# Attention: group 0's heads split behind block 1 of group 2, into places of used keys; input blocks 0 to 3 into places of the normed input

## The chip, the cores and the metric

The kernel runs on one core of a Trainium2 chip. The metric is the device time of one execution in microseconds (us). Before the change three runs took 1659.44, 1661.74 and 1659.78 us; the median is 1659.78 us.

The engines are named as in the profile: PE multiplies matrices (PEld is its weight load), DVE works on vectors, ACT computes functions of one argument and copies, POOL and SP issue DMAs here. Each engine runs its instructions in the order of its own program and waits on semaphores for the others.

## The reference

The program is the trunk of an encoder of two layers, over 768 tokens (512 of one request, 256 of another) of width 1024.

```python
for i in range(DEPTH):                      # 2 layers
    h = rms_norm(x, norm_mix[i])
    x = x + (window_attention(h, ...) if i % 2 == 0 else short_conv(h, ...))
    h = rms_norm(x, norm_mlp[i])
    x = x + jnp.square(jax.nn.relu(h @ mlp_w_up[i])) @ mlp_w_down[i]
    gate = jax.nn.sigmoid(rms_norm(x, norm_ple[i]) @ ple_w_gate[i])
    x = x + (p[i] @ ple_w_proj[i]) * gate
return rms_norm(x, final_norm)
```

`window_attention` has 16 heads in 4 groups with shared keys and values, each query sees the keys within 128 tokens, with a bias and a sink logit; its output is multiplied by `w_o`. The change touches the attention of layer 0, its output product and what follows it; `p[1] @ ple_w_proj[1]` of layer 1 is computed early, right behind that output product.

## The kernel before

**Numbers in two parts.** Every product is computed in fp32r from operands in two parts: `split(hi, lo, src)` writes the high part on ACT (L84) and the rest, `src - hi`, on DVE (L85). A term of a product is three matmuls: high weight by high input, high weight by low input, low weight by high input.

**Places.** Tokens lie along the free dimension, so a block of 128 channels is a tile of 128x768, 384 KB. Such tiles lie in numbered places, `slot(i, name)`. Taking a place again waits until the tile that had it before was last used. During the attention the places hold: 0, 1, 4, 8 the high and 2, 3, 5, 9 the low parts of the keys of groups 0 to 3 (`khh`, `kll`); 16 to 23 the high and 24 to 31 the low parts of the normed input (`xs_mix`), which the query products read; later the high (16 to 23) and low (24 to 31) parts of the attention's output, the split heads (`aos`); and 0 to 7 the eight blocks of the input x (`xa`), onto which the output product is added.

**Attention.** `attend(g)` runs over the groups g = 0 to 3 and in each over six blocks n of 128 queries. For a block: scores S on PE (L725, L726), bias and maximum on DVE (L727), exponential on ACT (L747), transposes `pt` (L760), probabilities in two parts `ph` (ACT, L768) and `pl` (DVE, L769), products O with the values (L770, L771), and the sum into `heads[g]` (DVE, L778). In this stage a scheduler sets the order of each engine's instructions from the order in which the program issues them and the times it reckons with. The table `beside` says which other work is issued behind block n of group g: query products for the heads to come (`queries(c)`), keys, layer 1's input, and, at (2, 4), `begin_output`: the heads of groups 0 and 1 are split. At (2, 5) `first_output` loads the first four blocks `xa` (L799) and forms the output products of groups 0 and 1 (matmuls L140 into `mm`, added by DVE at L794).

**Behind the attention.** `first_head` forms the output products of groups 2 and 3 for the eight blocks (matmuls L131), six of them in its loop in the order 4, 0, 5, 1, 6, 2, and adds each onto its block `xa[m]` to give x (DVE, L869). `first_tail` does blocks 7 and 3 and then the four products `pj` of layer 1's p (`product(m)`, L131). Their inputs, p in two parts for k = 0 and 1 (`p1`, the profile says `p`), are split in `second_inputs`: `behind(0)` and `behind(1)` take the places `xs0[24:]`, that is 16, 17 (high and low for k = 0), 18 and 19 (k = 1). Behind them comes the first MLP (L1096 and on), with products formed in seven multiplications in place of eight (L486). From `first_tail` on, PE, DVE and ACT keep the order in which the program is written.

Of the kernel before, what the change touches and what calls it, by code (L numbers as in the profile page):

```python
# [11 lines left out]
F32 = mybir.dt.float32  # L12
# [35 lines left out]
def trunk_kernel(ctx: ExitStack, tc: tile.TileContext, a: dict, out: bass.AP):  # L48
# [33 lines left out]
    def split(hi, lo, src):  # L82

        first = act.activation(hi, src, AF.Copy)  # L84
        dve.tensor_tensor(lo, src, hi.bitcast(F32), ALU.subtract)  # L85
        return first.ins
# [6 lines left out]
    def weight(src, n, raw=None, tag="w"):  # L93

        m = CH if src is None else src.shape[1]
        if raw is None:
            raw = fetch(src)
        pool, bufs = (wp, 2) if tag == "w" else (more, 1)
        hi, lo = (pool.tile([P, CH], F32R, tag=f"{tag}{p}", name=f"{tag}{p}", bufs=bufs) for p in ("hi", "lo"))
        split(hi[:, :m], lo[:, :m], raw[:, :m])  # L100
        return blocks(hi[:, :m], n), blocks(lo[:, :m], n)
# [48 lines left out]
    def slot(i, name, dt=F32R, n=T):  # L150

        return (slots if i < 32 else more).tile([P, n], dt, tag=f"S{i}", name=name)

    def big(name, dt=F32):

        nonlocal turn
        if more is None:
            return tmp.tile([P, T], dt, tag="t", name=name)
        turn += 1
        return tmp.tile([P, T], dt, tag=f"q{turn % 6}", name=name, bufs=1)  # L160

    def terms_of(w, xs, col=0):

        hi, lo = w
        c = slice(col, col + P)
        return [(wh[:, c], wl[:, c], xh, xl) for wh, wl, xh, xl in zip(hi, lo, *xs)]
# [324 lines left out]
    def mixer_attention():  # L491
# [25 lines left out]
        def products(terms):  # L517

            if not split_products:
                ps = psum.tile([P, 1024], F32, tag="mm", name="mm")  # L520
                group(ps, terms)
                yield ps[:, :T], 0, T
                return
            o = 0
            for i, n in enumerate(SEQS):
                ps = psum.tile([P, 512], F32, tag=f"mm{i}", name="mm", bufs=BM)
                group(ps, [(wh, wl, xh[:, o : o + n], xl[:, o : o + n]) for wh, wl, xh, xl in terms], n)
                yield ps[:, :n], o, o + n
                o += n
# [14 lines left out]
        with tc.manual_schedule(engines=order):  # L544
# [21 lines left out]
            hi = wp.tile([P, CH], F32R, name="whi", bufs=2)  # L566
            lo = wp.tile([P, CH], F32R, name="wlo", bufs=2)
# [25 lines left out]
        with s1:  # L593
# [29 lines left out]
            def queries(c):  # L623
                w = wq[0] if c == 0 else weight(a["w_q"][c], KB, raw=wq[1] if c == 1 else None)
                t = big("qt")
                for ps, o, e in products(terms_of(w, xs)):
                    dve.scalar_tensor_tensor(t[:, o:e], ps, HD**-0.5, r[:, o:e], ALU.mult, ALU.mult)
                hi = big("qh", F32R)
                lo = big("ql", F32R)
                split(hi[:], lo[:], t[:])  # L630
                for j in range(2):
                    h = 2 * c + j
                    qst[h] = slot(QS[h % 8], "q")
                    for i, part in enumerate((hi, lo)):
                        nc.sync.dma_start(
                            qst[h][64 * i : 64 * i + 64, :].bitcast(F32),
                            part[64 * j : 64 * j + 64, :].bitcast(F32),
                        )
# [11 lines left out]
            for i, raw in enumerate(rawv):  # L650

                m = min(T, 2 * CH - i * T)
                hi, lo = slot((4, 8, 10)[i], "wvh"), slot((5, 9, 11)[i], "wvl")
# [26 lines left out]
            aos = [], []  # L680
            xa = {}
# [100 lines left out]

            def split_heads(g):
                for i in range(2):
                    hi, lo = (slot(16 + 8 * p + 2 * g + i, "aos") for p in range(2))
                    split(hi[:], lo[:], heads[g][:, i, :])
                    aos[0].append(hi[:])
                    aos[1].append(lo[:])
# [6 lines left out]

            def load_part(m0):
                for m in range(m0, m0 + 4):
                    xa[m] = slot(m, "xa", F32)
                    nc.sync.dma_start(xa[m][:], a["x"][m])  # L799

            def first_output():
                load_part(0)
                for j in range(2):
                    w = weight(a["w_o0"][j], 4)
                    for i in range(2):
                        output_part(2 * j + i, w, i * P)

            def second_output():
                split_heads(2)
                load_part(4)  # L810
                for m in range(4, KB):
                    output_part(m, weight(a["w_o1"][m - 4], 6))
# [6 lines left out]
            def projected(n):  # L819
                if n == 0:  # L820
                    projw.append(weight(a["proj"][1, 0], 2))
                for m in range(2 * n, 2 * n + 2):
                    step(1, m, projw[0], part1, "t", False)
# [8 lines left out]
                    for p in range(2):  # L832
                        part1[p].append(ps[p][:, k, :])

            def begin_output():
                for g in range(2):
                    split_heads(g)


            beside = {  # L840
                (0, 5): (inputs1, keys1),
                (1, 4): (lambda: projected(0),),
                (1, 5): (lambda: projected(1),),
                (2, 4): (begin_output,),
                (2, 5): (first_output,),
            }
            for g in range(KV - 1):
                for n in range(2):
                    beside[g, 1 + 2 * n] = (lambda c=2 * g + 2 + n: queries(c),)
            for g in range(KV):  # L850
                attend(g)
            second_output()
            split_heads(3)
        return xa, aos

    xa, aos = mixer_attention()
    psum = ctx.enter_context(tc.tile_pool(name="ps", bufs=8, space=PSUM))
    more = ctx.enter_context(tc.tile_pool(name="more", bufs=1))
# [1126 lines left out]
```

## Time and profile before

| | |
|---|---|
| median of three runs | 1659.78 us |
| profiled execution, device time | 1661.51 us |
| its span in the trace | 1659.5 us |
| mean granted clock of PE over the span | 0.996 |
| busy: PE, DVE, ACT | 1637.6, 1380.8, 948.5 us |

The span runs from the first to the last instruction of the trace; 2.0 us of the device time lie around it. In rows of the timeline the columns are start (us), duration, engine, line, operation, tile written and tiles read, and in brackets the engine's idle time ahead of it with what ended it. Rows of windows give the stretch, its length, the busy time of each engine with the number of instructions, PE's granted clock (1.00 is full), the busy share of the DMA engines and GB/s. Rows of waits give who waited for whom: total us, times, the longest. The attention with the output products of groups 0 and 1 lies before 260 us, `first_head` and `first_tail` from about 268 to 303 us.

### The profile page before, as it was taken

To read this page: it belongs to the slowest core of one execution; us is meant where nothing else is said; L and a number is where in the kernel's file an instruction comes from. 1 tells how busy PE (TensorE), PEld (TensorE's weight loads), DVE (VectorE), ACT (ScalarE), POOL (GpSimd) and SP (SyncE) were. 2 spreads that over 40 slices of the span, in tenths; PEclk is the share of its full clock that TensorE was granted. 3 is DMA by queue.
4 is the path that set the end of the run, shared out by engine and by line. 5 is a ranking of instruction groups with operands and counts; after the bars stand their busy time and mean duration, and the time that the engine had idled before them with its cause. 6 is when DMAs were issued, how large, how long until landed. Compare 5 with 4: busy or idle time off the path is not lost.

```text
span 1659.5 us, 24297 instructions
## 1 busy us (share of the span) xinstructions
PE 1637.6 (99%) x9414; PEld 1587.3 (96%) x9414; DVE 1380.8 (83%) x2242; ACT 948.5 (57%) x1508; POOL 71.7 (4%) x104
## 2 busy tenths in 40 slices
PE   8999999999999999999999999999999999999997
PEld 7988789999999999999999999999999999999986
DVE  7598888898889889877888777778889888988776
ACT  7377766865556556545654434555555655655554
POOL 0211000000000000000000000000000000000000
PEclk9999999999999999999999999999999999999998
DMA  8755322443233333242312222112333323333222
GB/s 267 199 154 149 87 64 83 121 109 87 83 86 96 96 96 91 71 122 69 98 62 77 76 77 76 64 64 73 87 96 96 95 87 79 90 96 108 69 87 99
DMA packets 55476, 161.11 MB, mean 97 GB/s; under 512 B 7056, under 2 KB 10128, under 8 KB 55360
## 3 DMA queue, kind: packets, MB, share of 16 engines
q1 hardware_dynamic: 45184, 139.89, 26.4%
q0 software_dynamic: 10176, 19.67, 6.7%
q8 instruction: 74, 1.21, 0.3%
q14 instruction: 42, 0.34, 0.1%
HBM read 138.82 MB, written 10.48 MB: 90 GB/s over the span
## 4 chain that ended last, share of the span: by engine, by line
PE 88%; DVE 7%; ACT 4%; issue 1%; DMA 0%; DVEq 0%; SPq 0%; ACTq 0%
PE a L486 33%; PE mm L131 10%; PE mm L140 8%; PE b L486 8%; PE d L486 5%; PE c L486 5%; PE B L486 4%; PE C L486 4%; PE gate L140 3%; PE pt L760 1%; PE p L1096 1%; PE p L1199 1%; PE gate L131 1%; PE O L770 1%; PE O L771 1%
## 5 line engine op out<-in xcount | busy, mean ns | idle before, releaser
L486 PE MATMUL a<-xs,whi 128*128 128x384 f32 x624 | 121.8, 337 | 0.0
L444 ACT ACTIVATE vhi<-wraw 128x512 fp32r<-128x512 f32 x67 | 42.2, 631 | 132.3 <-PE B L486 87.9
L486 PEld LDWEIGHTS a<-xs,whi 128*128 128x128 f32 x624 | 110.0, 188 | 0.2 <-DVE y L1306 0.2
L486 PE MATMUL a<-t,zhi 128*128 128x384 f32 x536 | 109.1, 337 | 0.0
L486 PE MATMUL a<-t,whi 128*128 128x384 f32 x536 | 108.8, 336 | 0.0
L486 PE MATMUL b<-t,zhi 128*128 128x384 f32 x536 | 108.7, 336 | 0.0
L1341 DVE TENSOR_TENSOR x<-x,a 128x384 f32<-128x384 f32 x112 | 62.1, 554 | 55.3 <-PE a L486 55.3
L486 PE MATMUL a<-act,whi 128*128 128x384 f32 x448 | 96.5, 337 | 0.0
L486 PEld LDWEIGHTS a<-t,whi 128*128 128x128 f32 x536 | 94.9, 188 | 0.0
L486 PEld LDWEIGHTS b<-t,zhi 128*128 128x128 f32 x536 | 94.9, 188 | 0.0
L486 PEld LDWEIGHTS a<-t,zhi 128*128 128x128 f32 x536 | 94.8, 188 | 0.0
L464 DVE TENSOR_TENSOR wlo<-wraw,whi 128x1024 fp32r<-128x1024 f32 x70 | 85.2, 1218 | 7.9 <-ACT whi L444 7.9
L444 ACT ACTIVATE whi<-sum 128x1024 fp32r<-128x1024 f32 x67 | 70.6, 1054 | 27.0 <-PE a L486 22.7
L464 DVE TENSOR_TENSOR wlo<-sum,whi 128x1024 fp32r<-128x1024 f32 x67 | 81.8, 1220 | 5.1 <-ACT whi L444 5.1
L1058 ACT ACTIVATE y<-y 128x768 f32<-128x768 f32 x64 | 53.7, 839 | 54.4 <-DVE y L1055 54.3
L464 DVE TENSOR_TENSOR zlo<-sum,zhi 128x1024 fp32r<-128x1024 f32 x67 | 81.5, 1217 | 0.0
L140 PE MATMUL mm<-xs_mix,whi 128*128 128x512 f32 (+1 forms) x320 | 81.0, 341 | 0.0
L486 PEld LDWEIGHTS a<-act,whi 128*128 128x128 f32 x448 | 79.8, 188 | 0.0
L444 ACT ACTIVATE whi<-wraw 128x1024 fp32r<-128x1024 f32 x72 | 75.7, 1051 | 7.0 <-PE C L486 7.0
L444 ACT ACTIVATE zhi<-sum 128x1024 fp32r<-128x1024 f32 x67 | 70.9, 1058 | 11.9 <-DVE sum L420 11.0
L486 PE MATMUL a<-xs,wlo 128*128 128x384 f32 x312 | 67.1, 336 | 0.0
L358 ACT ACTIVATE t<-y 128x768 fp32r<-128x768 f32 x56 | 45.7, 838 | 34.9 <-DVE y L349 34.4
(345 smaller groups left out, 4558.4 us busy)
## 6 DMA issues: line engine op xcount, KB each, us to landing
wraw<-in_up SPq DMA_DIRECT2D x64, 512.0 KB, 3.9
wraw<-in_down SPq DMA_DIRECT2D x64, 512.0 KB, 4.2
wraw<-in_w_in SPq DMA_DIRECT2D x24, 512.0 KB, 3.5
wraw<-in_gate SPq DMA_DIRECT2D x16, 512.0 KB, 3.4
vlo<-in_up POOLq DMA_DIRECT2D x28, 256.0 KB, 5.6
vlo<-in_down POOLq DMA_DIRECT2D x28, 256.0 KB, 6.0
pj<-pjs SPq DMA_DIRECT2D x16, 384.0 KB, 2.8
wraw<-in_w_q SPq DMA_DIRECT2D x8, 512.0 KB, 4.6
```

Of the source, the lines that this page charges most:

```text
L131: pe.matmul(t, lhsT=w, rhs=x[:, o:e], start=first and i == 0 and j == 0, stop=last and i == n - 1 and j == 2)
L140: pe.matmul(ps[:, o:e], lhsT=w, rhs=x[:, o:e], start=i == 0 and j == 0, stop=i == n - 1 and j == 2,)
L358: act.activation(t[0][:], (self.q1, self.q2)[i][:], AF.Copy)
L444: act.activation(hi[:], src, AF.Copy)
L464: dve.tensor_tensor(lo[:], src, hi[:].bitcast(F32), ALU.subtract)
L486: pe.matmul(ps, lhsT=a, rhs=b, start=start and i == 0, stop=i == len(terms) - 1, skip_group_check=True)
L760: pe.transpose(pt[:, h * P : (h + 1) * P], lg[h // 2][:, h % 2, b * P : (b + 1) * P], ident[:],)
L770: pe.matmul(O[:], lhsT=v, rhs=ph[:], start=b == 0, stop=False)
L771: pe.matmul(O[:], lhsT=v, rhs=pl[:], start=False, stop=b == nk - 1)
L1058: act.activation(t[:], t[:], AF.Square)
L1096: pe.matmul(ps[o], lhsT=wt[:, c], rhs=xs[f"x{h + 1}{1 + o}"][m][part], start=k == 0 and j == 0, stop=k == KB - 1 and j == 2,)
L1341: dve.tensor_tensor(t[:, o : o + H], t[:, o : o + H], f, op)
```

## The change

Three edits. The split heads of group 0 go into places 0 and 1 (high) and 2 and 3 (low), those of the keys of groups 0 and 1, in place of 16, 17, 24 and 25. The blocks `xa[0]` to `xa[3]`, which had the places 0 to 3, go into 24, 25, 16 and 17. And group 0's heads are split by an entry of `beside` at (2, 1), behind `queries(6)`, and no longer at (2, 4), where group 1's stay. Lines behind L835 have numbers lower by 3 in the changed kernel.

```diff
             def split_heads(g):
                 for i in range(2):
-                    hi, lo = (slot(16 + 8 * p + 2 * g + i, "aos") for p in range(2))
+                    hi, lo = (slot(2 * p + i if g == 0 else 16 + 8 * p + 2 * g + i, "aos") for p in range(2))
                     split(hi[:], lo[:], heads[g][:, i, :])
...
             def load_part(m0):
                 for m in range(m0, m0 + 4):
-                    xa[m] = slot(m, "xa", F32)
+                    xa[m] = slot((24, 25, 16, 17, 4, 5, 6, 7)[m], "xa", F32)
                     nc.sync.dma_start(xa[m][:], a["x"][m])
...
-            def begin_output():
-                for g in range(2):
-                    split_heads(g)
-
...
-                (2, 4): (begin_output,),
+                (2, 4): (lambda: split_heads(1),),
                 (2, 5): (first_output,),
             }
             for g in range(KV - 1):
                 for n in range(2):
                     beside[g, 1 + 2 * n] = (lambda c=2 * g + 2 + n: queries(c),)
+            beside[2, 1] += (lambda: split_heads(0),)
```

How it moves instructions is seen at three places. First PE, where the output products begin, in group 2 of the attention. `aos_2502`, `2503`, `2506` and `2507` are the high and low parts of group 0's heads before, `aos_2236`, `2237`, `2240` and `2241` the same after; 2510 to 2515 are group 1's. Before:

```order
L771 MATMUL O_2344<-pl_2362,vv_457 128x512
L725 MATMUL S_2520<-khh_1388,q_1609 128x256
L726 MATMUL S_2520<-kll_1389,q_1609 128x256
L725 MATMUL S_2524<-khh_1388,q_1612 128x256
L726 MATMUL S_2524<-kll_1389,q_1612 128x256
L725 MATMUL S_2529<-khh_1388,q_1813 128x256
L726 MATMUL S_2529<-kll_1389,q_1813 128x256
L140 MATMUL mm_2594<-aos_2507,whi_2590 128x512
L140 MATMUL mm_2594<-aos_2506,wlo_2591 128x512
L140 MATMUL mm_2594<-aos_2510,whi_2590 128x512
```

After the change:

```order
L140 MATMUL mm_2594<-aos_2240,whi_2590 128x512
L140 MATMUL mm_2594<-aos_2241,whi_2590 128x512
L140 MATMUL mm_2594<-aos_2240,wlo_2591 128x512
L140 MATMUL mm_2594<-aos_2510,whi_2590 128x512
L725 MATMUL S_2463<-khh_1388,q_1816 128x256
L726 MATMUL S_2463<-kll_1389,q_1816 128x256
L140 MATMUL mm_2594<-aos_2511,whi_2590 128x512
L725 MATMUL S_2520<-khh_1388,q_1609 128x256
L726 MATMUL S_2520<-kll_1389,q_1609 128x256
L140 MATMUL mm_2594<-aos_2510,wlo_2591 128x512
```

Before, three pairs of scores stand ahead of the product with `aos_2507`; after, the product with `aos_2241` is in that run's place and scores and products alternate. Second, DVE early in the attention, where one of group 0's splits goes (piece of the difference):

```order
 L627 SCALAR_TENSOR_TENSOR qt<-mm,rstd_mix_428 128x512
 L755 TENSOR_SCALAR L<-L,sm 128x256 x3
+L85 TENSOR_TENSOR aos<-heads,aos 128x768
 L627 SCALAR_TENSOR_TENSOR qt<-mm,rstd_mix_428 128x256
 L769 TENSOR_TENSOR pl<-pt,ph 128x512 x2
```

The other goes some 100 instructions further on, ahead of the sums `sm`; where all four splits of groups 0 and 1 stood, group 1's two remain. Third, DVE in `first_head`, where the low part of `p1` for k = 0 (`p1_3369`) was written. Before:

```order
L794 TENSOR_TENSOR xa_3121<-xa_3121,mm_3267 128x512
L85 TENSOR_TENSOR zlo_3342<-wraw_3339,zhi_3341 128x1024
L85 TENSOR_TENSOR p1_3369<-wraw_3366,p1_3368 128x768
L794 TENSOR_TENSOR xa_3121<-xa_3121,mm_3287 128x256
L85 TENSOR_TENSOR wlo_3375<-wraw_3372,whi_3374 128x1024
```

After, in `first_tail`, where `xa_2586` is `xa[3]` and `xs7` and `x12` are the normed input of the MLP:

```order
L199 TENSOR_TENSOR acc_mlp0_3331<-acc_mlp0_3331,sq_3655 128x768
L866 TENSOR_TENSOR x_3328<-xa_2586,mm_3567 128x384
L866 TENSOR_TENSOR x_3328<-xa_2586,mm_3568 128x384
L85 TENSOR_TENSOR p1_3369<-wraw_3366,p1_3368 128x768
L308 SCALAR_TENSOR_TENSOR xs7_3668<-x_3328,vec_76,xs7_3668 128x384
L308 SCALAR_TENSOR_TENSOR x12_3669<-x_3328,vec_76,x12_3669 128x384
```

The split of `p1_3369` stands some 35 instructions later, behind the last add of the stage. On PE the products `pj` keep their place behind the output product of block 3; the first two read `p1_3368`, the next two `p1_3369`.

## The prediction

> **What bounds the kernel now.** I read the page first, then TensorE's waits over the whole run, then windows around the two stretches that the change touches.
>
> ```profile
> span 1659.5 us, 24297 instructions
> ...
> PE 1637.6 (99%) x9414; PEld 1587.3 (96%) x9414; DVE 1380.8 (83%) x2242; ACT 948.5 (57%) x1508; POOL 71.7 (4%) x104
> ...
> PE 88%; DVE 7%; ACT 4%; issue 1%; DMA 0%; DVEq 0%; SPq 0%; ACTq 0%
> ```
>
> PE is busy 99% of the span and carries 88% of the chain that ended last. The change leaves the number of instructions on every engine as it is, so only PE's idle time and PE's clock can move the end. All waits of PE together are few; these three stand in or near the stretches in question:
>
> ```profile
> PE mm L140 <- DVE aos L85: 1.6, 1, 1.6
> ...
> PE O L770 <- DVE heads L778: 0.4, 1, 0.4
> PE b L486 <- DVE zlo L464: 0.4, 1, 0.4
> ```
>
> The longest is PE waiting for the split of the heads (`aos`), once, for 1.6 us. Two-microsecond windows around it:
>
> ```profile
> 192.00:194.00 2.00, 2.00 (x16) 1.78 (x15) 2.00 (x6) 2.00 (x6) 0.00 (x0) 1.00 0.00 0
> 194.00:196.00 2.00, 2.00 (x15) 1.75 (x14) 2.00 (x6) 2.00 (x4) 0.00 (x0) 1.00 0.00 0
> 196.00:198.00 2.00, 1.58 (x13) 1.26 (x11) 1.96 (x6) 1.95 (x5) 0.00 (x0) 1.00 0.59 128
> 198.00:200.00 2.00, 1.84 (x6) 0.93 (x6) 2.00 (x7) 1.94 (x4) 0.00 (x0) 1.00 0.97 241
> 200.00:202.00 2.00, 0.93 (x6) 0.59 (x4) 1.88 (x7) 0.89 (x3) 0.00 (x0) 1.00 0.43 109
> 202.00:204.00 2.00, 1.52 (x4) 1.23 (x5) 2.00 (x3) 1.70 (x9) 0.00 (x0) 0.56 0.80 309
> 204.00:206.00 2.00, 2.00 (x9) 1.71 (x8) 2.00 (x11) 0.51 (x1) 0.00 (x0) 0.59 0.00 0
> ```
>
> Columns: length, then busy time of PE, PEld, DVE, ACT, POOL with counts, then PE's clock, the DMA share and GB/s. Two things are to be seen. PE idles 0.42 + 0.16 + 1.07 + 0.48 = 2.13 us between 196 and 204, while DVE is full from 192 to 206: here DVE is the bound. And the clock falls. Cut where it falls:
>
> ```profile
> 198.83:202.24 3.41, 2.10 (x9) 1.16 (x8) 3.29 (x12) 2.23 (x6) 0.00 (x0) 1.00 0.66 181
> 202.24:205.66 3.42, 3.18 (x9) 2.60 (x10) 3.42 (x12) 1.97 (x7) 0.00 (x0) 0.50 0.39 152
> ```
>
> After a stretch in which PE was idle for 1.3 of 3.41 us comes one of equal length at half clock, in which 3.18 us of PE's work took twice its time: 1.6 us lost. So what stands to be won here is about 2.13 + 1.6 = 3.7 us.
>
> **Part 1: group 0's heads split earlier (gain).**
>
> ```profile
> L85 DVE TENSOR_TENSOR aos<-heads,aos 128x768 fp32r<-128x768 f32 x4 | 3.6, 954 | 0.0
> ...
> 193.30 0.96 DVE L85 TENSOR_TENSOR aos<-heads,aos 128x768 fp32r<-128x768 f32 x1
> ...
> 201.47 2.69 DVE L85 TENSOR_TENSOR aos<-heads,aos 128x768 fp32r<-128x768 f32 x3
> ...
> 202.48 0.79 PE L140 MATMUL mm<-aos,whi 128*128 128x512 f32 x1 [1.56 <-DVE aos L85]
> ```
>
> Four low-part splits of 0.95 us each fall into 193 to 204, three of them back to back at 201.47, and PE resumes at 202.48 when the first of those three is done. After the change two of the four leave this stretch. In the new order they stand where DVE and ACT idle today:
>
> ```profile
> 123.00 0.51 ACT L747 ACTIVATE L<-L,nm 128x256 f32<-128x256 f32 x1 [1.11 <-DVE nm L740]
> ...
> 128.70 0.42 DVE L627 SCALAR_TENSOR_TENSOR qt<-mm,rstd_mix 128x256 f32<-128x256 f32 x1 [1.25 <-PE mm L140]
> ...
> 163.01 0.59 ACT L773 ACTIVATE ot<-O 64x512 f32<-64x512 f32 x1 [1.04 <-PE O L771]
> ...
> 173.14 0.69 DVE L627 SCALAR_TENSOR_TENSOR qt<-mm,rstd_mix 128x512 f32<-128x512 f32 x1 [1.73 <-PE mm L140]
> ```
>
> ACT's half of a split (0.84 us) fits its 1.11 and 1.04 us of idle, DVE's 0.95 us fits 1.25 and 1.73. I cost them at nothing there; without that cover each would hold the transposes behind it by up to 1 us. At 196 to 204 PE gets products of group 0 that wait for nothing, laid between its score products, and the idle before 202.48 goes. What is late next is DVE's own work there. From DVE's side the gain is 2 x 0.95 = 1.9 us, plus 1.6 if the clock then holds: 3.5. From PE's side it is at most 3.7. Following the new PE order with the durations of before, I come to 3.3, a score product still waiting about a microsecond for DVE to empty its bank. I take **-3.3**; ends -1.9 (the clock still falls) and -3.7.
>
> **Part 2: the first four input blocks are loaded later (nothing).**
>
> ```profile
> 188.07 0.40 PE L140 MATMUL mm<-xs_mix,whi 128*128 128x256 f32 x2
> ...
> DMA to landing us min/median/max: 3.1/3.7/6.9
> ...
> 195.64 0.46 SPq L635 DMA_DIRECT2D q<-qh  x1
> ...
> 207.19 0.68 DVE L794 TENSOR_TENSOR xa<-xa,mm 128x512 f32<-128x512 f32 x1
> ```
>
> The new places were held by the normed input, last read by the query products from 188.07 on. The four loads then follow on SP at about 189, ahead of the query copies that start at 195.64. The DMA share of 192 to 196 is 0.00 (windows above), so they land by about 196 even at 6.9 us. The first add into such a block was at 207.19. About 11 us of cover; if it were gone, each microsecond late would be one on the output sums, not at once on PE.
>
> **Part 3: what now stands in places 16 and 17 (loss).** Places 16 to 19 are taken over by the split second-layer input `p1` in `first_head`. Place 17 will hold `xa[3]`, which is read by the very last add of the stage (block 7 and block 3 come last; block 3 is at 297.01). So the low part of `p1`, k = 0, can no longer be written early.
>
> ```profile
> 268.22 0.85 ACT L84 ACTIVATE p<-wraw 128x768 fp32r<-128x768 f32 x1 [0.68 <-PE mm L140]
> ...
> 269.69 0.95 DVE L85 TENSOR_TENSOR p<-wraw,p 128x768 fp32r<-128x768 f32 x1
> ...
> 294.75 0.85 PE L131 MATMUL pj<-p,whi 128*128 128x384 f32 x4
> ...
> 297.01 1.01 DVE L869 TENSOR_TENSOR x<-xa,mm 128x384 f32<-128x384 f32 x2
> ...
> 299.44 0.62 DVE L308 SCALAR_TENSOR_TENSOR xs<-x,vec,xs 128x384 fp32r<-128x384 f32 x1 [1.42 <-ACT xs L307]
> ```
>
> DVE's split moves from 269.69 to behind the add of 297.01. It runs 298.02 to 298.97, inside the 1.42 us in which DVE waited anyway, so DVE loses nothing. ACT's high part (268.22) moves behind the add of block 2, near 289, where ACT idles up to 2.7 us per block. PE is another matter. Its products `pj` start at 294.75: two matmuls with the high part, 0.17 us apart, and then two with the low part. In order, PE stops at 295.1 until 299.0, and behind that stand the other `pj` products and everything of the MLP; nothing overtakes. Price: 299.0 - 295.1 = **+3.9 us**.
>
> What of it is given back? PE has hardly any idle time behind that place:
>
> ```profile
> 307.25 0.85 ACT L358 ACTIVATE t<-q 128x768 fp32r<-128x768 f32 x1
> ...
> 310.37 1.08 ACT L255 ACTIVATE ln<-ss,eps 128x384 f32<-128x384 f32 x2
> ...
> L238 PE MATMUL ss<-al,ones x2: 336/336/336, 307.5 to 307.8; 128*128 128x384 f32 x2
> ...
> 340.00:360.00 20.00, 19.62 (x112) 1.00 0.43 118
> 360.00:380.00 20.00, 20.00 (x117) 1.00 0.24 67
> ```
>
> ACT's chain waits for `ss`, which ended at about 308.1 and was read at 310.37, so ACT and DVE slip about 1.7 us where PE slips 3.9. The one stretch where PE later waits for them (340 to 360, 112 matmuls where a full window has 116) then closes: 4 x 0.173 = **-0.7**. From 360 on PE is full, and the slip stays to the end.
>
> **The clock in the new stall.** By the windows above, 1.3 us idle in a stretch of 3.41 brought half clock in the next. A stall of 3.9 us puts at least 1.9 us of idle into one such stretch, wherever their borders lie. If it fills one stretch, the next at half clock holds 0.5 us of the stall and costs (3.41 - 0.49) / 2 = 1.5. If it straddles two (2.6 and 1.3), both following stretches are halved: (3.41 - 1.3) / 2 + 3.41 / 2 = 2.8. I take **+1.5**; ends 0 and 2.8.
>
> The Trainium skill, "TensorE: Matmul & The Clock Gate", Part 1 (the HAM clock gate), gives the same free-running window of about 3.4 us, but has the clock fall after an idle window; by that letter a stall that straddles two windows leaves both partly busy, the term would be 0 and the sum -0.1 in place of +1.4. This trace speaks against the letter: its stretch at 198.83 was 62% busy and the next one was at 0.50.
>
> **Sum.** -3.3 + 0 + 3.9 - 0.7 + 1.5 = **+1.4 us**. The profiled execution took 1661.51 us (span 1659.5), so by its own time 1662.9. The median of the three runs is 1659.78, 1.7 lower, and the same difference on it gives **1661.2**.
>
> **Rivals.**
> - *Slower: the clock.* The halved stretch in the attention stays (DVE still full there, only the 1.9 us are won, 1.4 less), and the new stall straddles two stretches (2.8 in place of 1.5). It decides at about 1.3 us of idle within one stretch of 3.41. Sum -1.9 + 3.9 - 0.7 + 2.8 = +4.1: 1663.9. For it: DVE has no idle in 192 to 206, and 3.9 us is longer than a stretch. Against: three of the four idle pieces at 196 to 204 were behind splits that move.
> - *The clock holds in the stall.* If the stall leaves work in both stretches that it touches and this is enough, nothing is halved: -3.3 + 3.9 - 0.7 = -0.1, 1659.7, within 0.2%. For it: the trace has a single fall to judge by. Against: that one came with 62% of work in the stretch, more than the stall leaves in one of its two. The page named above would have it this way.
> - *Faster: the stall does not come, or comes short.* With no stall the gain stands alone: -3.3 to -3.7, about 1656.3; with half of it (1.95) and the clock held, -3.7 + 1.95 - 0.7 = -2.4, 1657.4. For it: DVE waits about 1 us for ACT in a block, so its adds could come a little earlier against PE. Against: the new order has the split behind the last add on DVE, and 297.01 stands at the end of a chain through ACT that the change leaves alone.
> - *The split is not moved at all.* The order on the engines shows that it is; the new places would leave the loss alone, +4.7. Under 3%, counted with slower.
>
> **How the numbers follow.** A measurement of this kernel can tell about 0.2%, 3.3 us, from no change: the bounds are 1656.5 and 1663.1. My forecast (+1.4, own range 1659.0 to 1663.0) gets 0.46, the clock that holds 0.17, both within: 0.63. Slower by the clock, with the unmoved split, 0.26; faster 0.11. The range goes from half a stall with the clock held (1657.4) over the forecast and the held clock to the slower rival and what the three runs lie apart above it (1663.9, rounded up by half their 2.3 us to 1665.0); beyond it remain the absent stall and the unmoved split.
>
> **What would show it.** Right: the wait for `aos` (1.6) is gone, PE is full and at clock 1.00 from 196 to 206, and in its place stands a wait "pj from DVE p" of about 3.9 us near 292 to 296, with a halved stretch behind it; the window of 20 us from 340 has 116 matmuls. Part 1 is wrong if PE's idle at 196 to 204 is replaced by waits for S or `pl`; part 3 is wrong if the wait at `pj` is under 3 us, and the clock term if PEclk behind it stays at 1.00. The prediction fails as a whole if the stall or the gain is off by 3 us, as would be the case if another engine's queue were held behind the late split.

## The result, and the profile after the change

| | before | after |
|---|---|---|
| median of 21 runs each | 1659.79 us (1658.99 to 1662.69) | 1663.75 us (1662.0 to 1664.69) |
| ratio, 95% interval | | 1.0021 [1.0014, 1.0027] |
| profiled execution, its span | 1661.51, 1659.5 us | 1664.69, 1662.7 us |
| mean granted clock of the profiled execution | 0.996 | 0.995 |

The changed kernel is slower: by 0.21% in the ratio over the runs, by 4.0 us (0.24%) at the median and by 3.2 us from one profiled execution to the other. The page of the changed kernel, and PE's waits:

```profile
PE 1639.2 (99%) x9414; PEld 1589.2 (96%) x9414; DVE 1380.6 (83%) x2242; ACT 948.5 (57%) x1508; POOL 72.0 (4%) x104
...
PE 92%; DVE 5%; ACT 1%; issue 1%; DMA 0%; DVEq 0%; SPq 0%; ACTq 0%
```

```profile
PE pj L131 <- DVE p L85: 3.8, 1, 3.8
...
PE S L725 <- DVE mx L727: 0.5, 1, 0.5
```

The wait for `aos` (1.6 us) is gone, a wait of 3.8 us for the split `p` has come, and what is left at the old place is 0.5 us for a score bank. The windows of the changed kernel in the attention (length, busy PE, PEld, DVE, ACT, POOL, clock, DMA share, GB/s):

```profile
196.00:198.00 2.00, 2.00 (x14) 1.75 (x13) 2.00 (x6) 1.95 (x4) 0.00 (x0) 1.00 0.30 77
198.00:200.00 2.00, 2.00 (x14) 1.80 (x14) 1.96 (x6) 1.06 (x2) 0.00 (x0) 1.00 0.99 237
200.00:202.00 2.00, 1.92 (x15) 1.59 (x13) 2.00 (x7) 0.60 (x1) 0.00 (x0) 1.00 0.92 226
202.00:204.00 2.00, 1.54 (x7) 1.14 (x8) 1.96 (x9) 1.06 (x5) 0.00 (x0) 1.00 0.78 215
204.00:206.00 2.00, 1.90 (x9) 1.39 (x10) 2.00 (x11) 1.69 (x9) 0.00 (x0) 1.00 0.72 178
```

PE is now idle for 0.64 us where it was idle for 2.13, the clock stays at 1.00, and DVE is as full as before (9.92 of these 10 us, before 9.84). The one wait of PE that is left there, 0.46 us at 203.43, is again for DVE. The timeline of the changed kernel where `first_tail` begins, PE and then DVE (start, duration, engine, line, operation, tiles, idle time ahead):

```profile
292.08 0.51 PE L131 MATMUL mm<-aos,wlo 128*128 128x384 f32 x2
292.42 0.51 PE L131 MATMUL pj<-p,whi 128*128 128x384 f32 x2
296.75 1.01 PE L131 MATMUL pj<-p,whi 128*128 128x384 f32 x2 [3.81 <-DVE p L85]
297.55 0.84 PE L131 MATMUL pj<-p,wlo 128*128 128x384 f32 x2
```

```profile
294.69 1.01 DVE L866 TENSOR_TENSOR x<-xa,mm 128x384 f32<-128x384 f32 x2
295.73 0.96 DVE L85 TENSOR_TENSOR p<-wraw,p 128x768 fp32r<-128x768 f32 x1
297.11 0.62 DVE L308 SCALAR_TENSOR_TENSOR xs<-x,vec,xs 128x384 fp32r<-128x384 f32 x1 [0.42 <-ACT xs L307]
```

PE does the two matmuls with the high part, then stands still until DVE has added the last block and split `p` behind it. DVE itself loses nothing: its next instruction waits for ACT anyway. And behind the wait two matmuls take 0.84 us where they took 0.51: the clock has fallen. Three stretches of 3.41 us of the same execution:

```profile
292.40:295.81 3.41, 0.54 (x4) 0.21 (x2) 2.89 (x5) 3.38 (x5) 0.00 (x0) 1.00 0.00 0
295.81:299.22 3.41, 2.47 (x8) 2.48 (x9) 2.99 (x4) 2.50 (x4) 0.96 (x1) 0.50 0.72 193
299.22:302.64 3.42, 3.42 (x12) 3.42 (x11) 2.01 (x4) 2.61 (x5) 0.00 (x0) 0.50 0.86 198
```

After the idle stretch not one but two come at half clock. From 296.75 to 302.64 PE does half of what it could: 5.89 / 2 = 2.9 us.

PE's matmuls are the same 9414 in both kernels, so the start of a matmul with the same number tells how far PE is. The 1040th (counted from 0) is a transposition of the attention, the 1690th belongs to the last output product, the 1745th to the first product of the MLP. The order on PE differs from the 985th to the 1242nd only; taken from the 980th, the first difference below would be -3.11 in place of -3.14. Matmuls that an experiment adds are left out of the count. Time from one to the next, worked out from the traces, in us:

```
                         1040 to 1690   1690 to 1745   1745 to 2100   2100 to end
before                   114.76          9.54          62.74          1292.84
after                    111.62         16.35          62.07          1292.24
difference                -3.14         +6.81          -0.67            -0.60
```

Up to the 1040th matmul the two executions differ by +0.8, and the sum is the 3.2 us of the spans. The -0.67 is the idle time of PE that the prediction saw at 340 to 360: the window has 116 matmuls now, before 112.

```profile
340.00:360.00 20.00, 20.00 (x116) 19.98 (x116) 18.05 (x26) 11.84 (x18) 1.50 (x2) 1.00 0.43 113
```

### The profile page after: what moved, and what is told of

The parts are those of the page before. It is cut to its first block, busy times and chain, and to the rows that moved or that the text cites. A ratio compares the mean times of both kernels' runs of the same rounds, so it can differ in the third digit from the quotient of the medians.

```text
span 1662.7 us, 24308 instructions
## 1 busy us (share of the span) xinstructions
PE 1639.2 (99%) x9414; PEld 1589.2 (96%) x9414; DVE 1380.6 (83%) x2242; ACT 948.5 (57%) x1508; POOL 72.0 (4%) x104
## 4 chain that ended last, share of the span: by engine, by line
PE 92%; DVE 5%; ACT 1%; issue 1%; DMA 0%; DVEq 0%; SPq 0%; ACTq 0%
PE a L486 34%; PE mm L131 9%; PE mm L140 9%; PE b L486 8%; PE d L486 5%; PE c L486 5%; PE B L486 4%; PE C L486 4%; PE gate L140 3%; PE p L1093 2%; PE p L1196 2%; PE pt L760 1%; PE gate L131 1%; PE O L770 1%; PE O L771 1%
```

## Experiments

**Only the places of `p1` altered.** Theory: the loss is the wait for place 17. The MLP's normed input takes 16 and 17 late, and `p1` for k = 0 takes 0 and 1.

```diff
-    xs0 = [*range(32, 42), *range(8, 15), *range(7), *range(16, 20)]
+    xs0 = [*range(32, 42), *range(8, 15), *range(2, 7), 16, 17, 0, 1, 18, 19]
```

> The change with one list altered: the numbers of places handed to the MLP's normed input end in 16, 17, and p1 for k = 0 gets 0 and 1, which the split heads of group 0 leave early. On PE and in the attention nothing differs from the change. Theory (the loss is the wait of pj for place 17, 3.8 us, with the clock behind it, 3.0 us, less 0.7 given back; the gain in the attention is 3.1): no wait of pj, clock 1.00 at 292 to 306, PE about 3.1 us ahead of before at 303, median near 1656.7 us, 0.998 of before. Rival (the later loads of the four input blocks or something else in the new order cost the time): the wait moves elsewhere and the time stays at 1660 or more.

Measured: 1657.27 us, ratio to before 0.998 [0.9971, 0.9989]. No wait of `pj` is left, and the windows of this kernel at the old place of the loss are full at full clock, while the small idle time at 340 to 360 is back:

```profile
280.00:300.00 20.00, 20.00 (x117) 20.00 (x117) 16.39 (x25) 13.21 (x19) 0.95 (x1) 1.00 0.28 69
340.00:360.00 20.00, 19.63 (x112) 19.11 (x111) 18.81 (x28) 12.50 (x18) 0.89 (x1) 1.00 0.26 70
```

In the steps above it takes 111.57, 9.54, 62.73 and 1291.55 us: the gain of the changed kernel (-3.2 against the traced execution of before), none of its loss. The late loads and the rest of the new order cost nothing that shows in these steps. This is the version to keep; it beats both. Its last step is 0.7 to 1.3 us shorter than in the other kernels. Against the kernel before at 1659.16 us, traced below, 0.8 us of this come in small pieces between 365 and 750 us and 0.2 near 1620 us; the kernel with one split below, which has like places, does the same (1291.49). The cause stays open. The expected 1656.7 was reached nearly, but by another sum: from the common runs of before in this comparison (1659.8 us, below) the gain in the attention is 1.7 and not 3.1, and the shorter last step, which no expectation had, gives 1.0 more.

**The entry in the table undone, the places kept.** Group 0 is split at (2, 4) again.

```diff
-                (2, 4): (lambda: split_heads(1),),
+                (2, 4): (lambda: split_heads(0), lambda: split_heads(1)),
...
-            beside[2, 1] += (lambda: split_heads(0),)
```

> The change's places, but group 0's heads are split at (2, 4) again, ahead of group 1's. Theory (the gain comes from when group 0 is split): the attention is as before, aos wait about 1.6 us and a halved stretch at about 202 to 206, and the pj wait of 3.8 us with one or two halved stretches stays: 3.8 + 1.5 to 3.0 - 0.7 over before, 1664.4 to 1665.9 us. Rival (the gain came from the places or the late loads): the attention stays about 3 us ahead of before, 1663.7 us.

Measured: 1664.33 us, ratio 1.002 [1.0011, 1.0029]. The number lies between the two, the trace decides: the theory falls. No wait for `aos` is left. Group 0's splits stand in DVE's timeline of this kernel as early as in the changed one (128.09 and 169.78 there):

```profile
127.80 0.95 DVE L85 TENSOR_TENSOR aos<-heads,aos 128x768 fp32r<-128x768 f32 x1
...
170.93 0.93 DVE L85 TENSOR_TENSOR aos<-heads,aos 128x768 fp32r<-128x768 f32 x1
```

The steps are 111.56 and 16.27 us, as after the change. With free places the scheduler puts both splits there, whichever of the two blocks of group 2 they are issued behind. So the third edit does nothing that these steps show once the first two are there; the free places bring the gain.

**The entry alone, the old places.**

```diff
-                (2, 4): (begin_output,),
+                (2, 4): (lambda: split_heads(1),),
...
+            beside[2, 1] += (lambda: split_heads(0),)
```

> The kernel before with the third edit alone: group 0's heads are split by the entry at (2, 1), but into the old places 16, 17, 24, 25, and the input blocks stay in 0 to 3. The splits can then not start before the query products behind 188 us have read these places. Theory (the places decide, the entry of the table does not): the splits come at about 189 to 192, still in the stretch where DVE is full, at most the 1.6 us wait for aos shrinks; no wait of pj; the typical run within 1.5 us of the kernel before. Rival (the entry decides): the gain of 2.4 to 3.3 us is here too, 1657.0 us.

Measured: 1659.3 us, ratio 0.9989 [0.998, 0.9998]. DVE's timeline has the two splits back to back, as soon as the places are free, and PE's wait for `aos` shrinks:

```profile
190.04 1.82 DVE L85 TENSOR_TENSOR aos<-heads,aos 128x768 fp32r<-128x768 f32 x2
```

```profile
PE mm L140 <- DVE aos L85: 0.5, 1, 0.5
```

The first step takes 112.27 us, 1.0 less than in those executions of before that have no halved stretch (113.2 to 113.3, below). The splits now fill a time in which DVE was idle: between 190 and 192 us it is busy for 2.00 us, in the kernel before for 0.77, so some of their work leaves the full stretch that follows. The median is 0.5 us below the lower of the two groups into which the runs of before fall (1659.78 us in this comparison; the groups are shown below), as the theory had it. Issuing the splits earlier is worth something with the old places, less than the new places give, and nothing on top of them.

**One of the two splits into new places.** On the kernel of the first experiment.

```diff
-                    hi, lo = (slot(2 * p + i if g == 0 else 16 + 8 * p + 2 * g + i, "aos") for p in range(2))
+                    hi, lo = (slot(2 * p if (g, i) == (0, 0) else 16 + 8 * p + 2 * g + i, "aos") for p in range(2))
...
-                    xa[m] = slot((24, 25, 16, 17, 4, 5, 6, 7)[m], "xa", F32)
+                    xa[m] = slot((24, 1, 16, 3, 4, 5, 6, 7)[m], "xa", F32)
...
-    xs0 = [*range(32, 42), *range(8, 15), *range(2, 7), 16, 17, 0, 1, 18, 19]
+    xs0 = [*range(32, 42), *range(8, 15), 1, 3, 4, 5, 6, 2, 16, 0, 17, 18, 19]
```

> The kernel of e1_p1_places, but only the first of group 0's two splits goes to places of used keys (0 and 2); the second stays in 17 and 25, and input blocks 1 and 3 in 1 and 3. So 0.95 us of DVE's work leave the full stretch in place of 1.9. Theory (DVE's work in that stretch sets PE's pace there): about half of the 3.2 us by which PE is ahead at 1200 matmuls, 1.2 to 2.0 us, median 1658.2 to 1658.8 us. Rival (only that the first output products find their operands ready counts): all of it, 1657.3 us, or none of it, 1659.7 us.

Measured: 1658.05 us, ratio 0.9981 [0.9972, 0.9991]. The first step takes 111.96 us, 2.8 less than in the traced execution of before, where half of 3.2 was expected. Neither theory fits that number. The last runs show one reason: 1.5 of the 3.2 us are a halved stretch, which many runs of before do not have and which does not come in halves; without it the gain is 1.3 of 1.7. The other is that the second split, though its places are the old ones, is not where it was before, among the three at 201.47:

```profile
191.48 0.95 DVE L85 TENSOR_TENSOR aos<-heads,aos 128x768 fp32r<-128x768 f32 x1
```

It has moved ahead, into the time in which DVE was idle, as in the run with the entry alone. So this run does not weigh one split against two.

**The clock alone.** The changed kernel with the wait filled: 24 matmuls that nobody reads.

```diff
-        def output(m):
-            ps = both()
+        def output(m, ps=None):
+            ps = ps or both()
...
+        output(m7, both("pj", "B"))
         pjs.extend(product(m) for m in range(KB // 2))
```

> The change with 24 more matmuls on PE between the last output product and pj (the output product of block 3 once more, into a bank of its own that nobody reads). They take 24 x 0.173 = 4.2 us and so fill the wait of 3.8 us. Theory (3.0 us of the loss are the clock that falls because PE idles): PEclk stays 1.00 at 292 to 306, no wait of pj over 0.2 us, and the sum is -3.1 + 4.2 - 0.7 = +0.4, near 1660.2 us. Rival (the clock term is not from the idle time, or the slow matmuls behind the wait have another reason): half clock stays and the time is that of the change or 0.4 more, 1663.7 to 1664.2 us.

Measured: 1662.37 us, ratio 1.001 [1.0001, 1.0019]. PE's timeline of this kernel has the added product up to the moment when `p` is there, and no idle time; its windows stay at full clock:

```profile
296.51 0.51 PE L131 MATMUL pj<-aos,wlo 128*128 128x384 f32 x2
296.86 0.85 PE L131 MATMUL pj<-p,whi 128*128 128x384 f32 x4
```

```profile
280.00:300.00 20.00, 20.00 (x118) 20.00 (x117) 16.00 (x26) 12.91 (x18) 0.59 (x1) 1.00 0.18 55
300.00:320.00 20.00, 20.00 (x116) 20.00 (x115) 16.26 (x24) 17.33 (x27) 0.37 (x1) 1.00 0.49 158
```

The second step takes 13.70 us, 9.54 and the 24 x 0.173 that were put in. PE does 4.2 us of useless work in place of a wait of 3.8 and is yet 2.65 us earlier at the MLP than in the changed kernel (16.35). So the clock is what the rest of the loss was. The total was expected at 1660.2 and is 2.2 us above it. That sum took a gain of 3.1 us from the median of before; against the runs without a halved stretch the gain is 1.7 (below), which makes 1.4 of the 2.2. The rest was not taken apart; the start alone differs by up to 2.5 us between executions of the same kernel.

**The wait alone.** The changed kernel with the k = 1 halves of three `pj` products put ahead.

```diff
+        def halves(ms):
...
-        pjs.extend(product(m) for m in range(KB // 2))
+        pjs.extend(product.halves(range(3)))
+        pjs.append(product(3))
```

`halves` forms the k = 1 halves of products 0, 1 and 2 and then their k = 0 halves.

> The change with the pj products put in another order: the k = 1 halves of the first three products (18 matmuls, 3.1 us), which need nothing that is late, come first, then their k = 0 halves, then the fourth product. Theory (nothing but p1's low part for k = 0 is waited for): the wait falls from 3.8 to about 0.7 us, the clock holds, PE is about 2.4 us ahead of before at 305, 1657.2 to 1657.6 us. Rival (PE would then wait for a bank that the last add has to empty, or the late split has cost on DVE and ACT too): a wait of 1.5 us or more stays or ss comes late, 1659 us or more.

Measured: 1658.84 us, ratio 0.9987 [0.9978, 0.9996]. PE's timeline has the wait shrunk by the 3.1 us that now lie ahead of it, and the clock holds:

```profile
294.50 0.51 PE L131 MATMUL pj<-p,whi 128*128 128x384 f32 x2
295.70 0.62 PE L131 MATMUL pj<-p,whi 128*128 128x384 f32 x2 [0.69 <-DVE p L85]
```

The second step takes 10.53 us (1.0 over before), the third 62.07 as after the change: a delay of only 1 us already closes the idle time at 340 to 360. The total is 1.2 us or more above the expected one, about what the same base makes (1.4).

**The kernel before, three times more, and the changed one.** The runs of before fall into two groups with nothing between: of 33 in one comparison, 18 at 1658.91 to 1660.17 us with a mean clock of 0.997 or more, 15 at 1661.54 to 1662.97 with 0.996. Of the 21 in the first table 14 are in the lower group and 7 in the upper, of 19 in a third comparison 9 and 10. The 21 runs of the changed kernel fall into two groups as well: 4 at 1662.0 to 1662.54 (0.996), 17 at 1663.39 to 1664.69 (0.995). One halved stretch is 3.41 / 2 / 1660 = 0.001 of the mean clock.

> The kernel before once more, for a trace of its commoner group of runs (18 of 33 at 1658.9 to 1660.2 us with a mean clock of 0.997, 15 at 1661.5 to 1663.0 with 0.996). Theory (the two groups differ by the phase of the clock's stretches): a run of the lower group has no halved stretch at 202 to 206, and its clock goes to full earlier than at 11.1 us; the wait for aos of 1.6 us is there as before. Rival (the groups differ by something else): a halved stretch in both.

> The kernel before once more, for a trace of the group of runs with a mean clock of 0.997. Theory: in such a run the wait for aos of 1.6 us is there, no stretch at 195 to 210 is halved, and from 190 to 225 PE loses about 1.7 us less than in the runs traced so far. Rival: the wait itself is shorter.

> As e8_before_third; a second chance for a trace of that group.

> The changed kernel once more, for a trace of its rarer group of runs (4 of 21 at 1662.0 to 1662.5 us with a mean clock of 0.996; 17 at 1663.4 to 1664.7 with 0.995). Theory (the number of halved stretches behind the wait for p makes the groups): a run with 0.996 has one halved stretch and loses about 1.5 us to it, one with 0.995 has two and loses about 3.0; the wait itself is 3.8 us in both. Rival: the wait is shorter in the rarer group.

Measured: 1662.96 us (a halved stretch from 204.91), 1659.16 and 1658.94 us (none), and 1662.94 us for the changed kernel (one stretch, from 297.38). The first fell into the upper group once more, so it is the next two that show the lower: no halved stretch, the clock full earlier, the wait still there, as the theory had it. The changed kernel waits 3.81 us in both of its executions, so the rival falls there too. In the second of these four, the kernel before at 1659.16 us, PE's wait and the windows are

```profile
PE mm L140 <- DVE aos L85: 1.5, 1, 1.5
```

```profile
200.00:202.00 2.00, 0.45 (x3) 0.25 (x3) 1.96 (x6) 1.02 (x5) 0.00 (x0) 1.00 0.65 190
202.00:204.00 2.00, 2.00 (x11) 1.74 (x12) 2.00 (x4) 1.16 (x6) 0.00 (x0) 1.00 0.51 203
204.00:206.00 2.00, 2.00 (x18) 1.92 (x17) 2.00 (x11) 0.59 (x2) 0.00 (x0) 1.00 0.15 31
```

The wait is the same and the clock does not fall. Steps of these executions beside those above:

```
                            1040 to 1690   1690 to 1745   halved stretches, clock full from
before, 1661.51 us           114.76          9.54          one     11.1 us
before, 1662.96 us           114.91          9.54          one     13.8
before, 1659.16 us           113.22          9.54          none     9.5
before, 1658.94 us           113.34          9.54          none     9.1
after, 1664.69 us            111.62         16.35          two     12.5
after, 1662.94 us            111.65         15.24          one     10.7
```

The last column is when the clock first went to full in that execution; the borders of the stretches follow from it: from there to the first half clock it is 191.15, 191.15, 283.31 and 286.72 us in the four that have one, which is 56, 56, 83 and 84 times 3.413 us. With it go the start (in the kernel before the 1040th matmul comes at 178.70 to 181.21 us) and the number of halved stretches. Between the two kinds of run of before that makes 1.5 us of the stretch and, in these four, 0.5 to 2.5 us of the start; the groups lie 2.4 us apart (1659.8 and 1662.2 us in the middle). The kernel with group 0 split late (1664.36 us, traced above) also has two halved stretches, from 295.23, and a mean clock of 0.995.

The changed kernel at 1662.94 us shows how one halved stretch comes about in place of two: a border falls in the middle of the wait, so that the stretch behind it is full of work.

```profile
290.56:293.97 3.41, 1.71 (x10) 1.39 (x9) 2.41 (x4) 2.72 (x4) 0.00 (x0) 1.00 0.00 0
293.97:297.38 3.41, 1.30 (x7) 1.30 (x8) 2.96 (x6) 3.38 (x5) 0.95 (x1) 1.00 0.39 131
297.38:300.79 3.41, 3.41 (x13) 3.41 (x12) 2.50 (x4) 2.31 (x5) 0.00 (x0) 0.50 0.88 202
```

## Why the prediction was right, and where it was off

The forecast was 1661.2 us, the measured median 1663.75: slower, as forecast, and inside the range (to 1665.0). The forecast's own bounds (to 1663.0) were missed, and the outcome held most likely did not come: no change beyond 3.3 us had 0.63, and +4.0 lies past that bound, in the part that had 0.26. The mechanism was right term by term; two sizes were off, the clock in the new stall and the base of the gain, and both made the forecast too low.

- **What bounds the kernel** was right: PE's idle time and clock moved the end, but for 0.6 us in the last step that was not followed up.
- **Part 1, -3.3 us:** -3.14 in the traced pair, so the sum was right for the execution it was made on. Its split into clock and DVE was close: two executions of before without the halved stretch put this stretch of the program 1.5 us lower (113.22 to 113.34 against 114.76 to 114.91), so the clock is 1.5 and the rest 1.6 to 1.7, where 1.6 and 1.9 stood. That the rest is DVE's relieved work is argued, not shown by a run of its own: the entry alone gives 1.0 of it while the wait for `aos` shrinks from 1.5 to 0.5, and there, too, DVE's work has moved into idle time. That the splits move because of the entry at (2, 1) was not claimed in the sum, but an expectation of mine rested on it, and it is wrong: with the new places the entry does nothing.
- **Part 2, nothing:** right; the four loads were issued from 189.26 us, and with `p1` elsewhere no trace of them is left.
- **Part 3, +3.9:** 3.81, at the place, by the engine and for the reason given. Counted as the prediction did, from when PE could have started its next matmul (292.77) to 296.75, it is 3.98. Given back, -0.7: 0.67.
- **The clock, +1.5:** mis-sized. Beyond the 3.81 it was 2.9 to 3.0 in the traced execution (2.8 beyond the 3.98), and by their mean clock 17 of 21 runs are like it; in the traced run with one halved stretch it was 1.9 (15.24 - 9.54 - 3.81; 1.7 beyond the stall as the prediction counts it). Two halved stretches, put at the upper end of 2.8, are the common case, though not by a stall that straddles two stretches: in the traced execution it fills nearly one, and what remains of it (0.94 us, from 295.81 to 296.75) left the next, halved one with 0.38 of the work that a full PE does, and another halved one followed.
- **The base:** "the same difference on it" failed as well. The gain was worked out on an execution with a halved stretch in the attention, 1.5 us of it was that stretch, and it was then set on a median of runs of which most have none. From typical run to typical run the terms are -1.6 + 3.8 + 3.0 - 0.7 = +4.5. The commoner groups fit: 1659.52 us in the middle of 14 runs before, 1663.97 of 17 after, +4.45. The medians of all runs show +4.0, the profiled pair 3.2.

The rivals: "slower: the clock" came close in number (1663.9) and half in kind. Two stretches behind the new wait are halved, but none stays in the attention after the change; that its small gain of 1.9 fits is luck, because most runs of before have no halved stretch there either. "The clock holds" was brought about by the filled wait, and there the steps follow it: -3.26 + 4.16 - 0.68 = +0.2 against the traced execution of before.

The reading of the threshold was wrong as well. I took 1.3 us of idle time in a stretch of 3.41 as enough. The execution of before at 1659.16 us, whose stretch was as busy by the profile (2.10 of 3.41 us had brought half clock), kept the clock:

```profile
200.64:204.05 3.41, 2.12 (x11) 1.86 (x12) 3.38 (x10) 2.18 (x9) 0.00 (x0) 1.00 0.63 224
```

Busy time of a matmul includes its modelled end; counted as columns at the pace of a full PE (0.173 us for 384) the stretches sort cleanly:

```
work in a stretch, share of it at full pace      the next stretch
before 1661.51: 0.34    before 1662.96: 0.36     half
after 1664.69: 0.11, then 0.38 (at half clock)   half, half
split late 1664.36: 0.19, then 0.32 (at half)    half, half
after 1662.94: 0.34                              half
after 1662.94, the stretch ahead of it: 0.46     full
before 1659.16: 0.59    before 1658.94: 0.60     full
```

The same count over every stretch of the twelve traces has no exception, if transposes and the last `ss` products are counted at their own pace (0.109 us for 128 columns, 0.215 for 256): at full clock, stretches with up to 0.36 were followed by half clock, those with 0.38 or more by full clock. At half clock in mid-kernel, 0.32 and 0.38 were followed by another halved stretch, 0.47 and more by full clock. This was worked out from the traces afterwards; no run was made to test it.

## What to carry to other kernels

A place (a buffer, a slot) that is freed early at one end is handed to the next user at the other: follow every later tenant of the places that a change swaps, up to the first engine that runs in order, before counting the gain. Where a scheduler orders the work, a free place can move an instruction further than the line that issues it: the new places alone moved the two splits from 193 and 201 us to 128 and 171, the new line alone to 190. And before a gain from one trace is set against a median, look whether that trace belongs to the common group of runs: here the mean clock to three digits told it.

## What the runs showed that was not expected

- The fall of the clock is a matter of chance for the same program: the kernel before idles 1.5 to 1.6 us for `aos` in every traced execution, and by their mean clock 15 of 33 runs lose another 1.5 us to a halved stretch. At full clock a stretch with 0.36 or less of the work of a full PE was followed by half clock, one with 0.38 or more was not.
- A stretch at half clock that still held 0.9 us of the stall was followed by a second one: a wait of 3.8 us cost 3.0 us more in that case, and 1.9 where only one stretch was halved.
- Twenty-four useless matmuls in the place of a wait made PE reach the next stage 2.65 us earlier than the wait itself.
